# Pacing a chunk inverse on VectorE against other work, and moving one matmul behind the next projection

## The chip, the cores and the metric

The kernel runs on one core of a Trainium2 chip. The metric is device time in microseconds (us) of one execution. The median of three runs is 1108.27 us (1107.01 to 1110.66). The execution that was profiled took 1108.38 us; the span from its first to its last instruction is 1106.6 us.

The engines are named as the profile names them: PE is the matmul engine (PEld its weight loads), DVE the vector engine, ACT the activation engine, POOL and SP the engines that here mostly issue transfers.

## The reference, cut to what matters

One layer of a hybrid encoder over 512 frames of width 1024. Three mixers run side by side (a gated short convolution, a gated linear recurrence, and an RWKV-7 time mixing with 16 heads of 64), their gated sum goes through an output matrix, and a squared-ReLU MLP follows. The part around the change is the RWKV-7 mixer:

```python
kk = heads(k * k_k)
kk = kk / jnp.maximum(jnp.sqrt(jnp.sum(kk * kk, axis=-1, keepdims=True)), 1e-12)
k = k * (1.0 + (a - 1.0) * k_a)
...
sa = jnp.einsum('bhvk,bhk->bhv', state, -kk_t)
state = (state * w_t[:, :, None, :]
         + sa[..., None] * (kk_t * a_t)[:, :, None, :]
         + v_t[..., None] * k_t[:, :, None, :])
y_t = jnp.einsum('bhvk,bhk->bhv', state, r_t)
```

`r`, `k` and `v` are projections of the normalized input, each mixed with its own value one frame earlier (the "token shift"). The sums in the second line are the key norms: one number for each head and frame.

## The kernel before, in words

Matmuls are made in three passes of a two-part split: every weight tile of 128x1024 is loaded by SP (`raw`), cast by ACT to its high part (`whi`, line 147) and subtracted by DVE to its low part (`wlo`, recorded at line 104, as all DVE `tensor_tensor` are). `scalar_tensor_tensor` is recorded at line 107. A projection (`proj`) takes one such weight tile and makes 8 x 3 matmuls of 512 columns (lines 168 to 170) into a bank of the PSUM pool `pp`, which has three. `raw` has two buffers, `whi` and `wlo` three each. Small results go to the PSUM pool `pm`, which has two banks for everything: norm sums `pn`, decay and gate products `pw` and `pa`, and the products `pG`, `pT` and others.

The recurrence is computed in chunks of 64 frames. The 16 heads are worked in four groups of four heads. For each group:

- `krv` (lines 416 to 509) makes the keys, receptances and values. It goes over two pairs of heads (`jj`), and for each it projects the key (`k`), shifts it into `ks`, squares it on ACT into `sq`, splits `sq` into `bh` and `bl`, multiplies them by a block-diagonal matrix of ones into `pn` (lines 433 and 434), and turns `pn` into `kk` by `rsqrt_rows`: a DVE transpose into `rqw` (line 194), some ten tiny operations on `rqq`, a transpose back (line 201) and a multiplication. Then it projects the receptance (`r`) and shifts it into `rs`; then come `pw` (lines 444 and 445), `pa` (450 and 451), a scan over frames, and the tiles `AR` and `BK`, which need `kk`, `rs` and `ks`. After both pairs come two value projections.
- `amat` (lines 515 to 542) multiplies `BK` with `AR` into 64x64 matrices for each chunk and head (`pA`, line 524), masks them into `AXt`, and transposes `BK` (`pB`, line 539).
- `inverse` (lines 544 to 599) inverts the triangular matrices of the group. It transposes two diagonal 32x32 blocks into a layout with one matrix for each partition (line 551, two transposes), then runs 31 dependent steps of two DVE operations each: a product into `dg` and a sum into `Z`. Two transposes bring the blocks back (line 573), one more prepares a left operand (line 578), then 2 x 16 small matmuls `pG` (line 585), 2 x 16 small matmuls `pT` (line 595) with ACT copies after each half, and the result goes to memory as `ttd`.

The order of the work is written out by generators. `weave(crit, fill, r)` advances `crit` by one `yield` and then `fill` by `r` yields on average, until `crit` ends. The critical generator is traced with a raised priority. For groups 1 to 3, `inverse` of the group before is the critical one and `fill_group` the filler; its steps are 22 steps of `ab` (the convolution and linear-recurrence mixers, one projection about every four steps), then the 26 steps of `krv` with 18 more `ab` steps mixed in, and 4 `ab` steps: 70 in all. What is left of them when `inverse` ends is run by `drain`; `amat` follows. The last group's `inverse` has plain `ab` steps beside it, and after it the chain over the chunks begins.

`inverse` yields 2 times before its steps, once after each step, `N_TT` times ahead of each of the three later transposes, `NINV` times ahead of `pG`, once after each half of `pG`, `NG_T` times ahead of `pT` and once after each half of `pT`.

A planner then fixes one order for each engine's queue: among the instructions that its own model takes to be ready it picks the one of highest priority, which is program order less the raise. `tc.keep_in_program_order(x)` ties an instruction to the one traced just before it on its engine, so that the planner cannot place it earlier. On the chip each queue runs in the order so fixed.

The constants are at lines 25, 28 to 31; `rsqrt_rows` at 190 to 201; the step that is tied at 562 to 564.

Of the kernel before, what the change touches and what calls it, by code (L numbers as in the profile page):

```python
# [9 lines left out]
F32 = mybir.dt.float32  # L10
# [8 lines left out]
P = 128  # L19
# [2 lines left out]
CP, CPV, CPI, CPC, CPN = 150, 20, 0, 20, 5  # L22
HOT = 6000

N_TT, NINV, NG_T, N_LOAD = 2, 7, 4, 6


N_KRV = 22
F_INV, F_KRV, F_GAP = 22, 16, 4
W3 = 3  # L30
R0, R1, R2, R3, R4 = 0.85, 0.87, 0.9, 1.7, 1.0
NWARM = 2
POOL_KT = (1, 3, 5, 6, 7)
S = 512
# [64 lines left out]
def block_kernel(ctx, tc, xt, win, par, mulr, sw, wout, w1, w2, fg, cst, eyes, out):  # L99
# [3 lines left out]
    def tt(o, a, b, op):  # L103
        return v.tensor_tensor(out=o, in0=a, in1=b, op=op)  # L104
# [9 lines left out]
    def f(t):  # L114
        return t.bitcast(F32)
# [14 lines left out]
    pv = lambda n, j: part[:, PI[n], j:j + 1]  # L130
# [28 lines left out]
    def split(pool, src, tag, rows=slice(0, P), bufs=None):  # L159
        th, tl = tag if type(tag) is tuple else (tag + "h", tag + "l")  # L160
        hi = pool.tile([P, S], F32R, tag=th, name=th, bufs=bufs)
        lo = pool.tile([P, S], F32R, tag=tl, name=tl, bufs=bufs)
        ac.copy(hi[rows], src)
        tt(lo[rows], src, f(hi[rows]), SUB)
        return hi, lo
# [21 lines left out]
            stt(t, t, -0.5, y, MUL, MUL)  # L187
            stt(y, t, 1.5, y, ADD, MUL)

    def rsqrt_rows(pool, o, ps, low, scale=1.0):  # L190

        w = pool.tile([P, S], F32, tag="rqw", name="rqw")
        q = pool.tile([P, 3, 16], F32, tag="rqq", name="rqq")
        v.transpose(w, ps)
        wv = w.rearrange("p (b j) -> p b j", j=32)[:, :, 0]
        if scale == 1.0:
            v.tensor_scalar(out=q[:, 0], in0=wv, scalar1=low, scalar2=None, op0=MAX)
        else:
            ts2(q[:, 0], wv, scale, low, MUL, ADD)
        rsqrt(q[:, 0], q[:, 1], q[:, 2])  # L200
        v.transpose(o, q[:, 1].unsqueeze(2).to_broadcast([P, 16, 32]))
# [9 lines left out]
    ps = ExitStack()  # L211
# [98 lines left out]
    def proj(name):  # L310
        w = load_w(win[CN[name]])
        t = pp.tile([P, S], F32, tag="pp", name="pp")
        for kt in range(KT):
            wh, wl = wslice(w, kt)
            mm3(t, wh, wl, hh[:, kt], hl[:, kt], start=kt == 0, stop=kt == KT - 1)
            if kt % 2 == 1 and kt < KT - 1:
                yield
        return t
# [5 lines left out]
    def shift(pt, mu, omu, o):  # L324
        ac.activation(o, pt, AF.Copy, scale=omu)
        stt(o[:, 1:], pt[:, 0:S - 1], mu, o[:, 1:], MUL, ADD)
# [3 lines left out]
    pk = pk_ctx.enter_context(tc.tile_pool(name="pk", bufs=1))  # L330
# [24 lines left out]
    OMK, OMR, OKA, OMV, N4, P4, HLG = range(7)  # L355
    v.tensor_scalar(out=dv[:, HLG], in0=part[:, PI["lg"]], scalar1=0.5, scalar2=None, op0=MUL)
    dvp = lambda i, j: dv[:, i, j:j + 1]
# [58 lines left out]
    def krv(g, G_):  # L416
        G_.AR = pk.tile([P, 2, NC, 2, L], F32, tag="AR", name="AR")
        G_.BK = pk.tile([P, 2, NC, 2, L], F32, tag="BK", name="BK")
        vs = [p1.tile([P, S], F32, tag=f"v{h}", name=f"v{h}") for h in range(2)]
        for jj in range(2):  # L420
            j = 2 * g + jj
            rs = WP("rs")
            if j == 0:
                ks = k0
            else:
                ks = WP("ks")
                t = yield from proj(("k", j))
                shift(t, pv("mu_k", j), dvp(OMK, j), ks)
            sq = WP("a1")
            ac.activation(sq, ks, AF.Square, scale=pv("kk", j))  # L430
            sqh, sql = split(pk, sq, "b")
            pn = pm.tile([P, S], F32, tag="pm", name="pn")
            pe.matmul(pn, bd, sqh, start=True, stop=False)
            pe.matmul(pn, bd, sql, start=False, stop=True)
            kk = WP("a5")
            rsqrt_rows(pk, kk, pn, 1e-24)
            stt(kk, ks, pv("kk", j), kk, MUL, MUL)
            yield
            t = yield from proj(("r", j))
            shift(t, pv("mu_r", j), dvp(OMR, j), rs)  # L440
            yield
            swh, swl = load_sw(pk, "swa", j, 0, 2)
            pw = pm.tile([P, S], F32, tag="pm", name="pw")
            pe.matmul(pw, swh[:, 0], lws, start=True, stop=False)
            pe.matmul(pw, swl[:, 0], lws, start=False, stop=True)
            sig = WP("a1")
            ac.activation(sig, pw, AF.Tanh, bias=pv("w0", j), scale=0.5)
            v.tensor_scalar(out=sig, in0=sig, scalar1=1.0, scalar2=None, op0=ADD)
            pa = pm.tile([P, S], F32, tag="pm", name="pa")
            pe.matmul(pa, swh[:, 1], las, start=True, stop=False)  # L450
            pe.matmul(pa, swl[:, 1], las, start=False, stop=True)
            av = WP("a4")
            ac.activation(av, pa, AF.Tanh, bias=pv("a0", j), scale=0.5)
            cum = WP("a2")
            v.tensor_tensor_scan(out=cum, data0=smk, data1=sig, initial=0.0, op0=MUL, op1=ADD)
            PP = pk.tile([P, NC, L + 1], F32, tag="PPt", name="PPt")
            gp.memset(PP[:, :, 0:1], 1.0)
            Pt = PP[:, :, 1:L + 1]
            ac.activation(Pt, c3(cum), AF.Exp, scale=-0.5 * CW)
            v.tensor_copy(PL[:, g, jj], PP[:, :, L])  # L460
            pinv = WP("a3")
            ac.activation(pinv, cum, AF.Exp, scale=0.5 * CW)
            stt(G_.AR[:, jj, :, 0], c3(kk), -1.0, PP[:, :, 0:L], MUL, MUL)
            tt(G_.AR[:, jj, :, 1], c3(rs), Pt, MUL)
            t_ = WP("a1")
            stt(t_, av, 1.0, kk, ADD, MUL)
            stt(G_.BK[:, jj, :, 0], c3(t_), 0.5, c3(pinv), MUL, MUL)
            kp = WP("a2")
            ts2(kp, av, pv("ka", j), dvp(OKA, j), MUL, ADD)
            tt(kp, kp, ks, MUL)  # L470
            tt(G_.BK[:, jj, :, 1], c3(kp), c3(pinv), MUL)

            if jj == 0:
                rk = [WP(f"rk{h}") for h in range(2)]
            for h in range(2):
                r = slice(64 * h, 64 * h + 64)
                stt(rk[h][64 * jj:64 * jj + 64], rs[r], part[r, PI["rk"], j:j + 1], kp[r], MUL, MUL)

        for jj in range(2):
            for h in range(2):  # L480
                gp.dma_start(axd[:, 0:64, g, 0, 2 * h + jj].rearrange("c d t -> d c t"),
                             G_.AR[64 * h:64 * h + 64, jj, :, 0])
            gp.dma_start(rtd[:, :, g, jj].rearrange("c p t -> p c t"), G_.AR[:, jj, :, 1])
        rk = [split(pk, rk[h], ("a1", "a3") if h else "b") for h in range(2)]
        for h in range(2):
            q = 2 * g + h
            t = yield from proj(("v", q))
            shift(t, pv("mu_v", q), dvp(OMV, q), vs[h])
            yield
        for h in range(2):  # L490
            pb = pm.tile([P, S], F32, tag="pm", name="pb")
            for i in range(2):
                pe.matmul(pb, bd, rk[h][i], start=i == 0, stop=i == 1)
            BV[2 * g + h] = [bv_tile(2 * g + h, th) for th in range(2)]
            for th in range(2):
                tt(BV[2 * g + h][th], pb[:, HALF[th]], vs[h][:, HALF[th]], MUL)
        yield
        for b in range(2):
            pt = pm.tile([P, 2, 2, P], F32, tag="pm", name="pV")
            for i in range(2):  # L500
                for h in range(2):
                    pe.transpose(pt[:, i, h], vs[h][:, (2 * b + i) * P:(2 * b + i + 1) * P], ident)
            vt = p1.tile([P, 2, 2, P], F32, tag="vt", name="vt", bufs=2)
            ac.copy(vt, pt)
            for i in range(2):
                c = 2 * (2 * b + i)
                gp.dma_start(vtd[c:c + 2, :, g].rearrange("c s e v -> (c s) (e v)"),
                             vt[:, i].rearrange("p h x -> p (h x)"))
        yield
# [34 lines left out]
    def inverse(g, G_):  # L544
# [12 lines left out]
        for s in range(31):  # L557
            n, c = 31 - s, s + 1
            tv = tmp[:, 0:n * c].rearrange("l (c t) -> l c t", c=c)
            mm = tt(tv, la[:, s, s + 1:32].unsqueeze(1).to_broadcast([64, c, n]),  # L560
                    xt[:, 0:c, s:s + 1].to_broadcast([64, c, n]), MUL)
            if s % 6 == 5:

                tc.keep_in_program_order(mm)
            tt(xt[:, 0:c, s + 1:32], xt[:, 0:c, s + 1:32], tv, ADD)
            yield
# [399 lines left out]
    with tc.tile_pool(name="mw", bufs=2) as mw, \  # L966
# [12 lines left out]
        for fi in range(NF):  # L979
            t = pp.tile([P, S], F32, tag="pp", name="p1")  # L980
            w = load_w(w1[fi])
# [7 lines left out]
            r = mw.tile([P, S], F32, tag="r", name="r")  # L989
# [18 lines left out]
        with tc.tile_pool(name="fin", bufs=1, side="right") as fin:  # L1008
# [15 lines left out]
            for fi in range(NF - 2):  # L1024
                w = load_w(w2[fi])
# [103 lines left out]
```

## Time and profile before

| what | value |
|---|---|
| median of three runs | 1108.27 us |
| profiled execution | 1108.38 us, span 1106.6 us |
| PE busy | 1056.1 us (95% of the span) |
| DVE busy | 743.6 us (67%) |
| ACT busy | 473.9 us (43%) |
| first `amat` begins | 97.8 us |
| second, third, fourth `amat` begin | 222.5, 350.9, 473.0 us |
| last small matmuls of the last `inverse` | 557 to 561 us |

The stretches between those starts are called group 1 (98 to 222.5 us), group 2 (to 350.9) and group 3 (to 473) below; the stretch to 562 us is the last group's. The chain over the chunks and the gates follow to about 676 us, the output matrix to 722 us, and the MLP to the end.

Rows of the view by stretches give the stretch, its length, then busy time and number of instructions for PE, PEld, DVE, ACT and POOL, then the granted PE clock as a share of full speed, the share of the transfer engines and GB/s. Rows of the view of waits read: engine and instruction, what it waited for, idle us in total, times, longest. Rows of the timeline give start, duration, engine, line, operation, tiles, shape and, in brackets, idle time ahead of it and what ended it. Rows of groups give busy us and mean ns of one, then idle time before.

### The profile page before, as it was taken

How to read it: one execution, taken by the hardware profiler on the slowest of the kernel's cores; microseconds unless marked ns; L12 is line 12 of the kernel's file. 1: busy time of each engine (PE TensorE's matmuls, PEld its weight loads, DVE VectorE, ACT ScalarE, POOL GpSimd, SP SyncE). 2: the span in 40 equal slices, each digit the busy share in tenths (PEclk: the TensorE clock that was granted, in tenths of full speed). 3: DMA queues.
4: the chain of work that ended last, by engine and by line, in shares of the span. 5: the costliest groups of instructions: out<-in, count | busy, mean ns of one | idle time of the engine just before them, and what ended most of it. 6: DMA issues, size and time to landing. Idle time of an engine off the chain costs nothing.

```text
span 1106.6 us, 16112 instructions
## 1 busy us (share of the span) xinstructions
PE 1056.1 (95%) x6396; PEld 865.3 (78%) x6396; DVE 743.6 (67%) x1276; ACT 473.9 (43%) x698; POOL 108.9 (10%) x167
## 2 busy tenths in 40 slices
PE   8899979999799989999899999999999999999996
PEld 5677868887588867887687887898888888888885
DVE  7997898879978998769947677955444443222224
ACT  6655445454344534534555444334433333221114
POOL 3211000210011101210022220001000000000001
PEclk9899989999989989999999999999999999999999
DMA  6243623562234623553279773234333335322231
GB/s 209 83 124 98 180 79 113 139 182 86 77 105 129 177 85 96 147 148 106 79 225 281 263 223 101 87 124 153 96 99 98 104 99 191 96 95 95 96 95 76
DMA packets 43324, 142.13 MB, mean 128 GB/s; under 512 B 5681, under 2 KB 9265, under 8 KB 42225
## 3 DMA queue, kind: packets, MB, share of 16 engines
q1 hardware_dynamic: 29472, 91.02, 25.7%
q0 software_dynamic: 13056, 49.03, 15.9%
q8 instruction: 50, 0.82, 0.3%
q10 hardware_dynamic: 720, 1.05, 0.3%
q14 instruction: 26, 0.20, 0.1%
HBM read 115.91 MB, written 25.17 MB: 127 GB/s over the span
## 4 chain that ended last, share of the span: by engine, by line
PE 65%; DVE 21%; DMA 5%; issue 5%; ACT 3%; POOL 1%; SPq 0%; ACTq 0%; POOLq 0%; DVEq 0%
PE pp L168 8%; PE pp L169 7%; PE pp L170 7%; PE acc L170 6%; PE acc L168 6%; PE acc L169 6%; PE p L169 5%; PE p L168 5%; PE p L170 5%; DVE wlo L104 4%; DMA raw<-in_win 3%; DVE dg L104 2%; DVE Z L104 2%; DMA rt<-rtd 1%; DVE u L107 1%
## 5 line engine op out<-in xcount | busy, mean ns | idle before, releaser
L104 DVE TENSOR_TENSOR wlo<-raw,whi 128x1024 fp32r<-128x1024 f32 (+1 forms) x164 | 199.5, 1219 | 249.8 <-ACT whi L147 248.9
L147 ACT CAST whi<-raw 128x1024 fp32r<-128x1024 f32 (+1 forms) x164 | 169.6, 1036 | 326.9 <-PE acc L170 125.1
L168 PE MATMUL pp<-hh,whi 128*128 128x512 f32 x696 | 278.5, 401 | 7.2 <-DVE ks L107 4.6
L170 PE MATMUL pp<-hh,wlo 128*128 128x512 f32 x696 | 277.5, 399 | 7.6 <-DVE wlo L104 7.6
L169 PE MATMUL pp<-hl,whi 128*128 128x512 f32 x696 | 277.4, 399 | 2.8 <-DVE hl L107 2.8
L168 PEld LDWEIGHTS pp<-hh,whi 128*128 128x128 f32 x696 | 133.7, 192 | 38.6 <-DVE ks L107 5.0
L170 PEld LDWEIGHTS pp<-hh,wlo 128*128 128x128 f32 x696 | 133.8, 192 | 37.6 <-DVE wlo L104 9.6
L169 PEld LDWEIGHTS pp<-hl,whi 128*128 128x128 f32 x696 | 133.7, 192 | 30.9 <-DVE hl L107 3.2
L170 PE MATMUL p<-h2h,wlo 128*128 128x512 f32 (+1 forms) x264 | 101.4, 384 | 0.0
L168 PE MATMUL p<-h2h,whi 128*128 128x512 f32 (+1 forms) x264 | 101.3, 384 | 0.0
L169 PE MATMUL p<-h2l,whi 128*128 128x512 f32 (+1 forms) x264 | 101.1, 383 | 0.0
L168 PE MATMUL acc<-whi,ah 128*128 128x512 f32 x256 | 99.6, 389 | 0.0
L169 PE MATMUL acc<-wlo,ah 128*128 128x512 f32 x256 | 99.6, 389 | 0.0
L170 PE MATMUL acc<-whi,al 128*128 128x512 f32 x256 | 99.6, 389 | 0.0
L168 PEld LDWEIGHTS p<-h2h,whi 128*128 128x128 f32 x264 | 49.7, 188 | 9.6
L170 PEld LDWEIGHTS p<-h2h,wlo 128*128 128x128 f32 x264 | 49.6, 188 | 9.7
L169 PEld LDWEIGHTS p<-h2l,whi 128*128 128x128 f32 x264 | 49.6, 188 | 9.5
L170 PEld LDWEIGHTS acc<-whi,al 128*128 128x128 f32 x256 | 48.0, 188 | 10.1
L169 PEld LDWEIGHTS acc<-wlo,ah 128*128 128x128 f32 x256 | 48.0, 188 | 10.0
L168 PEld LDWEIGHTS acc<-whi,ah 128*128 128x128 f32 x256 | 48.0, 188 | 9.8
L104 DVE TENSOR_TENSOR Z<-Z,dg 64x31 f32<-64x31 f32 (+15 forms) x124 | 42.2, 340 | 4.1
L104 DVE TENSOR_TENSOR dg<-Z 64x31 f32<-64x31 f32 (+15 forms) x124 | 42.2, 340 | 4.0
(296 smaller groups left out, 1457.0 us busy)
## 6 DMA issues: line engine op xcount, KB each, us to landing
raw<-in_win SPq DMA_DIRECT2D x88, 512.0 KB, 3.6
raw<-in_w SPq DMA_DIRECT2D x64, 512.0 KB, 3.5
ax<-axd POOLq DMA_DIRECT2D x8, 1024.0 KB, 7.2
axd<-AXt POOLq DMA_DIRECT2D x12, 512.0 KB, 7.2
bkd<-BKT POOLq DMA_DIRECT2D x4, 1024.0 KB, 13.6
raw<-in_wout SPq DMA_DIRECT2D x8, 512.0 KB, 4.3
bk<-bkd POOLq DMA_DIRECT2D x7, 512.0 KB, 8.0
swr<-in_sw SPq DMA_DIRECT2D x16, 128.0 KB, 2.3
```

Source lines behind the costliest of these rows:

```text
L104: return v.tensor_tensor(out=o, in0=a, in1=b, op=op)
L107: return v.scalar_tensor_tensor(out=o, in0=a, scalar=s, in1=b, op0=op0, op1=op1)
L147: ac.copy(hi[:, sl], raw[:, sl])
L168: pe.matmul(ps, wh, xh, start=start, stop=False)
L169: pe.matmul(ps, wh, xl, start=False, stop=False)
L170: pe.matmul(ps, wl, xh, start=False, stop=stop)
```

## The change

`N_TT`, `NINV` and `NG_T` become smaller and the ratios `R1` (groups 1 to 3) and `R2` (last group) larger: `inverse` yields fewer times, and more filler steps go by for each of its yields. In groups 1 to 3 it goes from 54 yields x 0.87 = 47 of the 70 filler steps to 47 x 1.2 = 56; in the last group from 54 x 0.9 = 48.6 to 47 x 1.02 = 47.9. Every third of its 31 steps, instead of every sixth, is tied to program order. In `krv`, the two matmuls `pn` and the `rsqrt_rows` behind them are traced after the receptance's projection and shift instead of ahead of them. `rsqrt_rows` takes the buffer tag of its wide scratch tile as an argument, and `krv` gives it `a3`, which is otherwise `pinv`'s.

```diff
-N_TT, NINV, NG_T, N_LOAD = 2, 7, 4, 6
+N_TT, NINV, NG_T, N_LOAD = 1, 4, 3, 6
-R0, R1, R2, R3, R4 = 0.85, 0.87, 0.9, 1.7, 1.0
+R0, R1, R2, R3, R4 = 0.85, 1.2, 1.02, 1.7, 1.0
-    def rsqrt_rows(pool, o, ps, low, scale=1.0):
+    def rsqrt_rows(pool, o, ps, low, scale=1.0, tag="rqw"):
-        w = pool.tile([P, S], F32, tag="rqw", name="rqw")
+        w = pool.tile([P, S], F32, tag=tag, name="rqw")
...
             sqh, sql = split(pk, sq, "b")
+            yield
+            t = yield from proj(("r", j))
+            shift(t, pv("mu_r", j), dvp(OMR, j), rs)
             pn = pm.tile([P, S], F32, tag="pm", name="pn")
             pe.matmul(pn, bd, sqh, start=True, stop=False)
             pe.matmul(pn, bd, sql, start=False, stop=True)
             kk = WP("a5")
-            rsqrt_rows(pk, kk, pn, 1e-24)
+            rsqrt_rows(pk, kk, pn, 1e-24, tag="a3")
             stt(kk, ks, pv("kk", j), kk, MUL, MUL)
-            yield
-            t = yield from proj(("r", j))
-            shift(t, pv("mu_r", j), dvp(OMR, j), rs)
             yield
...
-            if s % 6 == 5:
+            if s % 3 == 2:
                 tc.keep_in_program_order(mm)
```

## The prediction

> **What bounds the kernel now.** I read the page first, then the view by stretches, to see where PE is not busy.
>
> ```profile
> span 1106.6 us, 16112 instructions
> ...
> PE 1056.1 (95%) x6396; PEld 865.3 (78%) x6396; DVE 743.6 (67%) x1276; ACT 473.9 (43%) x698; POOL 108.9 (10%) x167
> ```
> ```profile
> 98.00:222.50 124.50, 116.50 (x658) 94.52 (x656) 110.44 (x197) 58.42 (x85) 15.05 (x24) 0.97 0.44 123
> 222.50:350.90 128.40, 118.96 (x659) 97.09 (x658) 108.39 (x195) 60.62 (x89) 11.85 (x18) 0.95 0.40 113
> 350.90:473.00 122.10, 117.02 (x659) 95.50 (x658) 104.97 (x188) 54.45 (x78) 14.44 (x22) 0.96 0.45 126
> 473.00:562.00 89.00, 83.14 (x512) 67.01 (x512) 75.65 (x127) 44.27 (x63) 4.11 (x6) 0.98 0.39 114
> 722.00:1092.00 370.00, 370.00 (x1763) 311.30 (x1763) 137.93 (x155) 114.52 (x156) 6.98 (x11) 1.00 0.33 106
> ```
>
> The MLP (last row) has no idle PE and a full clock; nothing there can move. In groups 1 to 3 and the last group PE is idle for 8.0 + 9.4 + 5.1 + 5.9 = 28.4 us, and the clock is below full. DVE is busy for 85 to 89% there, far above its 67% over the span: two engines are near their bound at once. The waits say what PE stood for:
>
> ```profile
> PE pn L433 <- ACT bh L163: 9.4, 4, 5.3
> PE pp L170 <- DVE wlo L104: 7.6, 4, 5.8
> PE pp L168 <- DVE ks L107: 4.6, 1, 4.6
> PE pB L539 <- DVE AXt L104: 1.8, 2, 1.6
> PE pp L168 <- ACT g L797: 1.4, 1, 1.4
> PE pG L585 <- DVE u L789: 1.2, 1, 1.2
> DVE rqw L194 <- PE pn L434: 3.9, 4, 1.4
> ```
>
> The first row names ACT, but the timeline shows that DVE was the late one:
>
> ```profile
> 155.08 0.67 ACT L325 ACTIVATE ks<-pp,dv 128x512 f32<-128x512 f32 x1
> ```
> ```profile
> 110.77 2.11 DVE L551 STREAM_TRANSPOSE Z<-AXt 32x1024 f32<-32x1024 f32 x1
> ...
> 155.85 1.23 DVE L104 TENSOR_TENSOR wlo<-raw,whi 128x1024 fp32r<-128x1024 f32 x1
> 157.11 0.21 DVE L104 TENSOR_TENSOR Z<-Z,dg 64x31 f32<-64x31 f32 x1
> 157.35 1.90 DVE L573 STREAM_TRANSPOSE Z<-Z 32x1024 f32<-32x1024 f32 x1
> 159.28 0.69 DVE L104 TENSOR_TENSOR u<-u,g 128x512 f32<-128x512 f32 x1
> 159.88 0.74 DVE L107 SCALAR_TENSOR_TENSOR ks<-pp,part,ks 128x511 f32<-128x511 f32 x1
> ...
> 163.85 1.23 DVE L578 STREAM_TRANSPOSE dg<-Z 32x1024 f32<-32x1024 f32 x1
> ```
> ```profile
> 162.15 0.80 PE L433 MATMUL pn<-bh,bd 128*128 128x512 f32 x1 [5.34 <-ACT bh L163]
> ```
>
> ACT had its half of the key's shift at 155.75; DVE took it up at 159.88, 4.1 us later, behind the inverse's last step and a transpose. `pn` needs that shift, a square and a cast, so PE stood for 5.34 us. The idle time has a second price, the clock in the stretch right after each stall (PE busy without a break, clock in the column before the last two):
>
> ```profile
> 162.15:168.00 5.85, 5.85 (x16) 4.66 (x17) 5.52 (x16) 2.72 (x4) 0.00 (x0) 0.60 0.00 0
> 279.40:284.00 4.60, 4.60 (x13) 3.70 (x14) 3.75 (x7) 1.53 (x2) 0.00 (x0) 0.63 0.07 27
> 304.82:315.00 10.18, 10.18 (x82) 8.36 (x83) 7.10 (x10) 2.56 (x4) 0.00 (x0) 0.57 0.37 116
> 408.31:414.00 5.69, 5.69 (x16) 4.55 (x17) 5.37 (x11) 1.69 (x3) 0.00 (x0) 0.63 0.54 179
> 438.00:445.00 7.00, 7.00 (x51) 5.50 (x50) 5.88 (x16) 3.24 (x5) 0.71 (x1) 0.76 0.39 76
> 546.60:554.00 7.40, 7.39 (x80) 6.27 (x81) 7.10 (x9) 4.53 (x6) 0.00 (x0) 0.77 0.32 102
> ```
>
> Length times the missing share gives 2.3 + 1.7 + 4.4 + 2.1 + 1.7 + 1.7 = 13.9 us. Groups 1 to 3 thus lose 22.5 us idle, less some 2 us ahead of `pB` and its like that no edit touches, and 12.2 us of clock: 32.7 us are in reach. The last group loses 5.9 + 1.7.
>
> **The change part by part: the spread.** What it moves is DVE work:
>
> ```profile
> L104 DVE TENSOR_TENSOR dg<-Z 64x31 f32<-64x31 f32 (+15 forms) x124 | 42.2, 340 | 4.0
> L104 DVE TENSOR_TENSOR Z<-Z,dg 64x31 f32<-64x31 f32 (+15 forms) x124 | 42.2, 340 | 4.1
> ```
> ```profile
> 175.77 2.14 PE pG L585 x64
> ...
> 222.59 1.99 PE pA L524 x32
> ```
>
> A step is two operations of 0.34 us with some 0.03 us ahead of each (4.0 us / 124): 0.74 us, and 31 steps are 23 us for each group. Two transposes of line 573 and one of line 578 add about 5 us. From the end of the line 551 transposes (112.88) to `pA` (222.59) are 109.7 us for 70 filler steps, 1.57 us each.
>
> Before, step s stands after 0.87 (s + 2) filler steps, so all 31 are through at 28.7, the three transposes at 34. After, the steps end at 33 x 1.2 = 39.6 and the transposes at 43. At filler step 22, where `krv` begins, 23 steps were traced before and 16 will be: 7 x 0.74 = 5.2 us less. At step 35, when the first pair's key and receptance are projected, it is 31 against 27 steps and the three transposes: 3 + 5 = 8 us less DVE work ahead of what PE needs. The stalls in those places are 5.8 us and less. What is late next is the same 8 us, now at steps 36 to 43, beside the second pair. The room for them:
>
> ```profile
> 163.00:222.00 59.00, 59.00 (x361) 47.99 (x361) 51.31 (x93) 31.33 (x45) 9.91 (x16) 0.97 0.44 123
> 313.00:350.00 37.00, 36.73 (x217) 29.80 (x217) 30.02 (x55) 23.24 (x35) 5.13 (x8) 0.99 0.43 118
> ```
>
> DVE idles 7.7 and 7.0 us there; less 0.03 us for each instruction, 4.9 and 5.3 us are usable. So about five of eight fit, not all in the right place. I take half of the 32.7 us as kept, for both edits of groups 1 to 3 together: -16.4 us. Bounds: none of it, if the stalls only move back; or four fifths, -26 us. DVE's own floor does not forbid that: its busy time and the 0.03 us gaps come to 116, 114 and 111 us for stretches of 124.5, 128.4 and 122.1.
>
> The ties make runs of three steps (2.2 us) where six (4.4 us) could stand; a tied step waits behind whatever filler work was traced ahead of it on DVE, and the steps behind it wait too. Nobody waits for those steps before `pG`, so this costs nothing while `pG` has slack. That slack shrinks: `NINV` 7 x 0.87 = 6.1 filler steps become 4 x 1.2 = 4.8, or 2 us less; in group 1 it is 10.7 us (165.08 to 175.77). In the last group 6.3 become 4.1, 3.5 us less, and there PE already waited 1.2 us at `pG`. Between 0 and 2 us in each group and 0 and 3.5 us in the last; I take +1 in all for the former and +2 for the latter. The spread itself is only 12% thinner in the last group (steps end at 33.7 instead of 29.7): -1.5 of its 7.6 us.
>
> **The norm sums.** Removed is PE's wait for the chain shift, square, cast: 9.4 us. Its cover is the receptance's 24 matmuls at 0.23 us, 5.5 us, longer than the longest wait. The cover needs its weights: in group 1 their split ended at 157.08, 0.3 us after PE stopped. This saving is within the half already taken, because DVE is late next. Added is a wait: `pn`, `pw` and `pa` now follow one another at once on the two banks of `pm`, so `pa` waits until DVE has transposed `pn`, and PE's queue stands behind it. Bounds: 0, and the 4.1 us of lag that DVE had at `ks`. The nearest row is `rqw` itself: DVE waited for PE there four times in eight, so it is mostly prompt. I take 0.3 us for eight pairs, +2.4. The `rsqrt_rows` chain is late by a projection, hidden by the value projections between it and `amat`. The tag `a3` costs nothing: its other users come behind `rqw` on DVE's own queue. No transfer is added, and SP's loads keep their traced order (`k`, `r`, the small weights). POOL issues the stores of `AR` later, since `kk` is later; what reads them is loaded only for the chain after 562 us.
>
> **The clock.** The stretch from 438 us stands behind a stall of 0.47 us, that from 546.6 behind those of 1.4 and 1.2 us at `g` and `pG` in the waits, and both have a reduced clock:
>
> ```profile
> 435.92 0.50 PE L433 MATMUL pn<-bh,bd 128*128 128x512 f32 x1 [0.47 <-ACT bh L163]
> ```
>
> So short stalls count too, and halving them gives back about half. The Trainium skill (TensorE: Matmul & The Clock Gate, section "Why this matters for your kernels") says to avoid idle gaps over about 3 us; by that alone, gaps halved to under 3 us would give all the lost clock back. The trace disagrees in the two rows above.
>
> **Sum:** -16.4 - 1.5 + 1 + 2 + 2.4 = -12.5 us on the profiled execution's 1108.38 (0.1 us from the median): 1096 us.
>
> **The rivals.**
> - DVE is the bound: the moved 8 us push stalls from the first pair to the second and to `amat`. For it: 85 to 89% busy. Against it: the usable idle time above. The gain would be 0 to 5 us: 1104 to 1108, say 1106.
> - Slower: `pa` waits for `pn`'s bank. If DVE is as late at `rqw` as it was at `ks`, 4.1 us for the six pairs of groups 1 to 3 is 24.6 us against 14.9 of gain: 1118. It decides from 2.5 us for each pair. Against it: DVE's promptness at `rqw` so far; for it: 8 us more DVE work in that very place.
> - The clock returns whole, because halved stalls no longer trip it: another 6.1 us, 1090. Against it: the two rows above. This is the rule of the Trainium skill cited above.
> - The spread does not happen, since the planner reorders, and only `pn` is moved: half of 9.4 + 4.0, 1102. Against it: 28.7 steps x 1.57 = 45 us, and the steps did take 44.4 us (112.88 to 157.32): program order is followed.
>
> **How the numbers follow.** Forecast 0.47, DVE bound 0.20, slower 0.18, clock 0.08, no spread 0.07. About 0.3% (3.3 us) is what a measurement of this kernel can tell. The forecast, the clock and no spread are faster, and a third of the DVE rival: 0.69; its rest is the same: 0.13; slower 0.18. The range goes from 1082 (the four fifths, with nothing else) to 1113, half-way into the slower rival; about 0.15 is left out. The likeliest case's own range is 1084 to 1104.
>
> **What would show it.** Right: the row of `pn` falls under 2 us in all; from line 551 to the last step some 62 us pass in each group instead of 44; the three stretches shorten to about 119, 121 and 119 us; fewer stretches at half clock. Wrong: a new row of `pa` or `pw` waiting for `rqw` or ACT; waits at `pA` or `AXt` of several us; `pG` waiting for line 578 by more than 2 us; DVE above 95% busy with PE idle as before.

## The result, and the profile after

The changed kernel takes 1116.97 us (median of eight runs, 1110.83 to 1119.52) against 1108.17 us for the kernel before in the same measurement: a ratio of 1.0074 [1.0052, 1.0096]. It is slower by 8.8 us, where 12.5 us less were forecast. The profiled execution took 1118.59 us, with this page:

```profile
span 1116.8 us, 16116 instructions
...
PE 1059.4 (95%) x6396; PEld 867.1 (78%) x6396; DVE 741.9 (66%) x1276; ACT 473.2 (42%) x698; POOL 107.7 (10%) x167
```

The page hides the change: the same work, the same shares. The view by stretches does not. The stretches are again cut at the starts of `amat`, and the last one at the end of the last small matmuls (568.30 us; before, the cut at 562 lies 0.7 us behind that end):

```profile
98.20:227.60 129.40, 121.34 (x659) 97.47 (x658) 110.03 (x197) 58.44 (x85) 15.29 (x25) 0.95 0.41 119
227.60:345.40 117.80, 114.25 (x660) 92.98 (x659) 106.07 (x194) 60.24 (x89) 10.75 (x17) 1.00 0.43 123
345.40:473.80 128.40, 119.98 (x659) 97.47 (x658) 104.36 (x189) 55.03 (x78) 15.14 (x24) 0.93 0.41 120
473.80:568.30 94.50, 82.26 (x504) 66.23 (x503) 75.50 (x127) 42.99 (x62) 4.10 (x6) 0.93 0.36 107
```

Length less the second number is PE's idle time; length times what the clock lacks is the time lost to the clock. Both are worked out so below, for the rows of before too; the clock is given to two places, so a figure of the last column is good to some 0.6 us.

| stretch | length before, after | PE idle before, after | lost to the clock before, after |
|---|---|---|---|
| group 1 | 124.5, 129.4 | 8.0, 8.1 | 3.7, 6.5 |
| group 2 | 128.4, 117.8 | 9.4, 3.6 | 6.4, 0.0 |
| group 3 | 122.1, 128.4 | 5.1, 8.4 | 4.9, 9.0 |
| last group | 89.0, 94.5 | 5.9, 12.2 | 1.8, 6.6 |
| sum | | 28.4, 32.3 | 16.8, 22.1 |

Group 2 gained more than forecast, 10.6 us. Groups 1 and 3 and the last group lost more than that together: the last `amat` begins 375.3 us after the first before, and 375.6 us with the change. The mark for what the last group costs is the chain's first matmul that reads the recurrent state (`py<-St,rt`, line 652), here before and after:

```profile
588.06 1.15 PE L652 MATMUL py<-St,rt 64*64 64x64 f32 x32 [1.54 <-DMA rt<-rtd]
598.04 1.15 PE L652 MATMUL py<-St,rt 64*64 64x64 f32 x32 [1.36 <-DMA rt<-rtd]
```

It comes 115.0 us after the start of the last `amat` before and 124.2 us with the change, so the last group costs 9.2 us; from there to the end both take about the same, 518.5 and 518.8 us. Idle time rose by 3.9 us and lost clock by 5.3, 9.2 us of the 10.2 by which the span grew.

What PE stood for now:

```profile
PE pG L585 <- DVE dg L578: 16.2, 3, 10.8
PE pp L168 <- DVE ks L107: 5.8, 1, 5.8
PE pa L450 <- DVE rqw L194: 3.7, 2, 1.9
...
PE pB L539 <- DVE AXt L104: 1.8, 2, 1.6
PE pn L436 <- ACT bh L163: 1.7, 3, 0.7
```

The rows that led before, `pn` with 9.4 us and `wlo` with 7.6, are down to 1.7 and 1.1 us. In their place leads a row that the kernel before did not have: `pG` waits 16.2 us, 10.8 of them at once, for the transpose of line 578, the last piece of the inverse on DVE. Before, `pG` waited 1.2 us in all, in the last group; its row names `u`, a tiny operation of DVE that ends together with that transpose:

```profile
545.33 1.23 DVE L578 STREAM_TRANSPOSE dg<-Z 32x1024 f32<-32x1024 f32 x1
546.61 2.21 PE L585 MATMUL pG<-dg,AXt 32*32 32x32 f32 x64 [1.16 <-DVE u L789]
```

The timeline of PE in the last group shows the place after the change:

```profile
547.35 0.39 PE L169 MATMUL pp<-hl,whi 128*128 128x512 f32 x1
558.50 3.62 PE L585 MATMUL pG<-dg,AXt 32*32 32x32 f32 x64 [10.76 <-DVE dg L578]
562.04 0.80 PE L170 MATMUL pp<-hh,wlo 128*128 128x512 f32 x1
```

And that of DVE in the same stretch, with the weight split that the projection needs (`wlo` at 545.96), the inverse's last steps (`dg` and `Z`, shapes shrinking to 64x31) and its three transposes:

```profile
535.75 0.32 DVE L104 TENSOR_TENSOR Z<-Z,dg 64x156 f32<-64x156 f32 x1
536.10 0.69 DVE L107 SCALAR_TENSOR_TENSOR u<-u,u 128x512 f32<-128x512 f32 x1
...
545.96 1.20 DVE L104 TENSOR_TENSOR wlo<-raw,whi 128x1024 fp32r<-128x1024 f32 x1
547.07 0.68 DVE L107 SCALAR_TENSOR_TENSOR g<-g,u 128x512 f32<-128x512 f32 x1
547.77 0.30 DVE L104 TENSOR_TENSOR dg<-Z 64x135 f32<-64x135 f32 x1
...
553.11 0.21 DVE L104 TENSOR_TENSOR Z<-Z,dg 64x31 f32<-64x31 f32 x1
553.35 3.83 DVE L573 STREAM_TRANSPOSE Z<-Z 32x1024 f32<-32x1024 f32 x2
557.21 1.23 DVE L578 STREAM_TRANSPOSE dg<-Z 32x1024 f32<-32x1024 f32 x1
```

The inverse stops for 11.7 us in the middle of its steps (536.07 to 547.77) while DVE works on the filler (and idles for some 2.5 us in between), and goes on 0.02 us after a filler operation ends. That step is the 27th, one of those that the change ties. PE has come to `pG` at 547.74 and stands there, in the middle of a projection: line 170, which follows `pG` in its queue, has had its weights since 547.16. The Trainium skill (PSUM — Partial Sum Buffer, section "Engine vs sequencer instructions") says that matmuls start and complete in program order; the trace agrees, for the ready matmul ran at 562.04, behind all of `pG`.

Each such stall is followed by a reduced clock, again with PE busy nearly throughout (the first two rows; the third holds the rest of the stall at `ks` as well, the fourth that of 2.56 us at `pG`):

```profile
193.70:206.00 12.30, 12.28 (x114) 9.86 (x115) 7.76 (x21) 4.56 (x8) 0.68 (x1) 0.60 0.05 12
558.50:566.00 7.50, 7.50 (x103) 6.39 (x103) 4.19 (x6) 1.87 (x3) 0.55 (x1) 0.58 0.31 107
398.20:408.00 9.80, 4.03 (x11) 3.24 (x11) 9.36 (x19) 1.71 (x3) 0.00 (x0) 0.65 0.23 69
432.70:442.00 9.30, 6.74 (x72) 5.57 (x72) 7.72 (x11) 4.32 (x7) 0.00 (x0) 0.63 0.42 144
```

The first row stands behind a wait of 2.84 us at `pG` in group 1 and costs 4.9 us of clock (12.3 x 0.40): more than the wait itself, and as much as the whole of group 1 grew by.

### The profile page after: what moved, and what is told of

It reads as the page before. It is cut to its first block, busy times and chain, and to the rows that moved or that the text cites. A ratio compares the mean times of both kernels' runs of the same rounds, so it can differ in the third digit from the quotient of the medians.

```text
span 1116.8 us, 16116 instructions
## 1 busy us (share of the span) xinstructions
PE 1059.4 (95%) x6396; PEld 867.1 (78%) x6396; DVE 741.9 (66%) x1276; ACT 473.2 (42%) x698; POOL 107.7 (10%) x167
## 4 chain that ended last, share of the span: by engine, by line
PE 62%; DVE 23%; DMA 5%; issue 5%; ACT 3%; POOL 1%; SPq 0%; DVEq 0%; ACTq 0%; POOLq 0%
PE acc L169 7%; PE pp L168 7%; PE acc L170 7%; PE acc L168 7%; PE pp L169 6%; PE pp L170 6%; PE p L170 5%; PE p L169 5%; PE p L168 5%; DVE wlo L104 5%; DVE dg L104 3%; DVE Z L104 3%; DMA rt<-rtd 2%; DMA raw<-in_win 2%; DVE Z L573 1%
## 6 DMA issues: line engine op xcount, KB each, us to landing
swr<-in_sw SPq DMA_DIRECT2D x16, 128.0 KB, 2.2
```

## The experiments

After the result there were two theories for the 10.8 us. The first: the tie of every third step holds the inverse behind filler work that was traced ahead of it, so DVE finishes late. The rival: the thinner pace (larger ratio, fewer yields) sets `pG` too early against DVE, whatever the ties. Beside them stood the question what the norm sums' move is worth by itself. All ratios below are to the kernel before, measured beside each run on the same chip; "the old settings" are those of before.

### The parts by themselves: the norm sums

The kernel before, with only the norm sums moved.

```diff
# the changed kernel, with the settings of before
+N_TT, NINV, NG_T, N_LOAD = 2, 7, 4, 6
+R0, R1, R2, R3, R4 = 0.85, 0.87, 0.9, 1.7, 1.0
+            if s % 6 == 5:
```

> The kernel before with only the norm sums moved behind the receptance; all constants and ties as before. Theory 1 and 2: the waits at pn (9.4 us) go, some of it comes back elsewhere: 1098 to 1106 us. Theory 3 (PE waits at pa for pn's bank): 1112 us or more, with waits at pa of over 8 us in all.

Measured: 1107.17 us, 0.999 [0.9976, 1.0004]: no difference that counts, though the wait that it aims at is gone. Its leading waits:

```profile
PE pa L450 <- DVE rqw L194: 5.8, 3, 3.2
PE pp L168 <- DVE ks L107: 5.2, 2, 4.6
```

With the old pace the waits at `pn` and `wlo` go (1.9 and 1.8 us are left), and others come: `pa` behind `pn`'s bank takes 5.8 us where there was none, and `pG` 2.2 us for the transpose of line 578. `ks` keeps its place. The three groups last 124.0, 128.0 and 122.0 us, within half a microsecond of before.

### The parts by themselves: the spread

The kernel before with the change's constants and ties, the norm sums left in their old place; and the same for groups 1 to 3 alone, with the last group as before.

```diff
# spread only, on the kernel before
+N_TT, NINV, NG_T, N_LOAD = 1, 4, 3, 6
+R0, R1, R2, R3, R4 = 0.85, 1.2, 1.02, 1.7, 1.0
+            if s % 3 == 2:
# spread in groups 1 to 3 only, on the kernel before
+R0, R1, R2, R3, R4 = 0.85, 1.2, 0.9, 1.7, 1.0
+        N_TT, NINV, NG_T = (2, 7, 4) if g == NG - 1 else (1, 4, 3)
+            if (s % 6 == 5) if g == NG - 1 else (s % 3 == 2):
```

> The changed constants and ties, with the norm sums where they were before. Theory 1 and 2: the wait at pG in the last group stays about 10 us, time 1114 to 1122 us. Theory 3: no loss, 1108 us or less.

> The kernel before with only groups 1 to 3 spread (yields 1, 4, 3, ratio 1.2, every third step tied); last group and norm sums as before. If the two edits work on the same stalls independently: 1109 to 1112 us (the norm sums alone gave 1 us). If the spread needs the moved norm sums, because the key's chain now competes with the inverse for longer: 1115 to 1120 us, with waits of several us at pn in groups 1 and 3.

Measured: 1127.37 us, 1.0172 [1.0149, 1.0194], and 1118.27 us, 1.0071 [1.0055, 1.0088]. Without the moved norm sums the spread saves nothing. The waits of PE in the second of these:

```profile
PE pn L433 <- ACT bh L163: 8.3, 5, 4.3
PE pp L170 <- DVE wlo L104: 6.8, 5, 4.6
PE pp L168 <- DVE ks L107: 6.5, 1, 6.5
```

`pn` and `wlo` keep 8.3 and 6.8 us of their 9.4 and 7.6. So the two edits are not additive: the norm sums' move is worth 1 us alone (inside its interval), and 9 to 11 us beside the spread (1.0071 against the 0.9992 of the next experiment; 1.0172 against the whole change's 1.0074).

### Where the loss sits: the last group

The whole change, with the last group's inverse wholly as before; and the kernel before, with only the last group's inverse as changed.

```diff
# last group old, on the changed kernel
+R0, R1, R2, R3, R4 = 0.85, 1.2, 0.9, 1.7, 1.0
+        N_TT, NINV, NG_T = (2, 7, 4) if g == NG - 1 else (1, 4, 3)
+            if (s % 6 == 5) if g == NG - 1 else (s % 3 == 2):
# last group new, on the kernel before
+R0, R1, R2, R3, R4 = 0.85, 0.87, 1.02, 1.7, 1.0
+        N_TT, NINV, NG_T = (1, 4, 3) if g == NG - 1 else (2, 7, 4)
+            if (s % 3 == 2) if g == NG - 1 else (s % 6 == 5):
```

> The changed kernel with everything of the last group's inverse as before (yields 2, 7, 4, ratio 0.9, every sixth step tied); groups 1 to 3 and the norm sums as changed. If the last group alone holds the loss (theory of the last group): its wait at pG of 10.8 us falls to about 1 us, the chain starts some 9 us sooner, time 1105 to 1109 us. If the loss is spread over the groups: 1112 us or more.

> The kernel before with only the last group's inverse as changed (yields 1, 4, 3, ratio 1.02, every third step tied); norm sums and groups 1 to 3 as before. Theory of the last group: PE waits about 10 us at pG there, time 1116 to 1120 us. If the loss is spread over the groups: within 3 us of 1108.

Measured: 1108.97 us, 0.9992 [0.9978, 1.0006]; and 1118.94 us, 1.0071 [1.005, 1.0092]. The whole loss against before goes with the last group's new settings, and comes with them alone: there `pG` waits 10.8 us, as in the changed kernel (the profile of that run is of its shortest execution, 1113.19 us). With the last group old, `py` of line 652 comes 115.7 us behind the last `amat` (115.0 before, 124.2 with the change). What is left for groups 1 to 3 is nought: group 2's gain against the losses of the other two.

### Ties or pace

Four kernels. The whole change with the old ties (every sixth step); the whole change with the tie of the 27th step alone taken off in the last group; the last group with its old pace but the new ties (the rest as changed); and the whole change with the ties of the 25th and later steps, and those of the three transposes behind them, taken off.

```diff
# ties of before
-            if s % 3 == 2:
+            if s % 6 == 5:
# the 27th step loose
+            if s % 3 == 2 and not (g == NG - 1 and s == 26):
# last group: old pace, new ties
+R0, R1, R2, R3, R4 = 0.85, 1.2, 0.9, 1.7, 1.0
+        N_TT, NINV, NG_T = (2, 7, 4) if g == NG - 1 else (1, 4, 3)
# the whole tail loose
+            if s % 3 == 2 and s < 24:
-            tc.keep_in_program_order(v.transpose(TT[...], xt[...]))
+            v.transpose(TT[...], xt[...])
-        tc.keep_in_program_order(v.transpose(d1[0:32], TT[0:32, :, 0:32]))
+        v.transpose(d1[0:32], TT[0:32, :, 0:32])
```

> The changed kernel with the ties of before (every sixth step). Theory 1 (the tie): in the last group step 27 (the 5x27 product) is tied behind the gelu and scan block of the filler, 12 us late, and PE stands 10.8 us at pG and then runs some 10 us at half clock. With every sixth step tied that step is loose: the wait at pG in the last group falls under 2 us, and the time to 1102 to 1107 us. Theory 2 (the yields): pG comes too early because there are fewer yields ahead of it, whatever the ties: its wait in the last group stays over 6 us and the time over 1112. Theory 3 (the norm sums): the loss is at pn, pw and pa: the time stays at 1117.

> The changed kernel with one tie taken out: step 27 (the 5x27 product) of the last group; the order on the vector engine's queue is the changed kernel's up to that step. Theory 1: the whole loss of the last group is that tie: steps 27 to 31 and the three transposes end about 10 us earlier, PE's wait at pG there falls from 10.8 to under 2 us, the half clock behind it goes or is short, time 1102 to 1106 us. Theory 2: the wait at pG stays over 5 us and the time over 1111. Theory 3: 1117, as the changed kernel.

> The changed kernel with the last group's yields and ratio as before (2, 7, 4 and 0.9), every third step tied everywhere. PE's order is that of the run with the last group all old; only DVE's differs. If pace makes the last group's loss: the transposes are early again, wait at pG under 3 us, 1107 to 1111 us. If the ties alone make it: an early tied step stands behind a filler block, the inverse ends up to 8 us later, PE waits over 5 us at pG, 1113 or more.

> The changed kernel with the ties of the 25th and later steps and of the three later transposes taken out. Theory of the ties: the last steps and the transposes no longer stand behind filler work, the transpose of line 578 ends 5 to 12 us earlier, PE's waits at pG are under 3 us in all, time 1100 to 1107 us. Theory of the distance: the loose transposes are still placed by the planner near their traced place, the waits stay over 8 us in all, time 1112 or more.

Measured, in that order: 1114.94 us, 1.0058 [1.0039, 1.0078]; 1117.42 us, 1.0083 [1.0057, 1.0109]; 1120.7 us, 1.0088 [1.007, 1.0106]; 1105.38 us, 0.9954 [0.9938, 0.997].

With the old ties `pG` in the last group still waits 8.9 us, and `py` comes 124.3 us behind the last `amat`. So the first theory fell as it stood: the closer ties are not needed for the loss. There the steps end at 537.71, but the transpose of line 578, which was tied before the change too, starts only at 550.47. With only the 27th step loose it is the same: the steps end at 540.3, 13 us sooner than with the change, and the transpose of line 578 starts at 553.10:

```profile
540.13 0.21 DVE L104 TENSOR_TENSOR Z<-Z,dg 64x31 f32<-64x31 f32 x1
540.37 1.95 DVE L573 STREAM_TRANSPOSE Z<-Z 32x1024 f32<-32x1024 f32 x1
...
545.41 1.95 DVE L573 STREAM_TRANSPOSE Z<-Z 32x1024 f32<-32x1024 f32 x1
...
553.10 1.23 DVE L578 STREAM_TRANSPOSE dg<-Z 32x1024 f32<-32x1024 f32 x1
```

`pG` waits 8.9 us there: one tie taken off, and the next one of the same kind is what is late. The rival theory fell as well: at the old pace the new ties alone lose as much (`py` comes after 125.3 us), with the third step stuck behind a filler operation whose block waits for a late transfer (`swr`):

```profile
488.38 0.22 DVE L104 TENSOR_TENSOR Z<-Z,dg 64x60 f32<-64x60 f32 x1
...
497.97 0.29 DVE L104 TENSOR_TENSOR swcl<-swr,swch 128x128 fp32r<-128x128 f32 x1 [6.43 <-ACT swch L406]
...
506.12 0.74 DVE L107 SCALAR_TENSOR_TENSOR g<-g,part,g 128x510 f32<-128x510 f32 x1
506.89 0.25 DVE L104 TENSOR_TENSOR dg<-Z 64x87 f32<-64x87 f32 x1
```

From 488.6 to 506.89 the inverse does not move, and DVE idles 6.43 us of that; `pG` waits 9.9 us at the end. In the kernel before, the steps went on around the same wait (at 491.54 its sixth step was done). With the whole tail loose the loss turns into a gain: line 578 starts at 540.71 there, and `pG` waits 6.2 us, since the planner now also places it earlier, at 535.8. The gain is that of groups 1 to 3, which take 368.7 us from the first `amat` to the last (375.3 before); the last group is still 5.3 us above before.

The times of the last group, in us from the start of its `amat`, show which side moved:

| kernel | PE comes to `pG` | line 578 ends | wait at `pG` | `py` of line 652 |
|---|---|---|---|---|
| before | 72.4 | 73.5 | 1.2 | 115.0 |
| the change | 73.9 | 84.6 | 10.8 | 124.2 |
| ties of before | 72.0 | 80.9 | 8.9 | 124.3 |
| the 27th step loose | 72.1 | 80.9 | 8.9 | 125.4 |
| old pace, new ties | 71.8 | 81.6 | 9.9 | 125.3 |
| the whole tail loose | 69.1 | 75.2 | 6.2 | 120.3 |

In the four kernels that lose all of it, PE is where it was to within 1.5 us, and DVE is 7 to 11 us later. Loosening the tail brings DVE back to within 2 us; what is left of the wait are these 2 us and PE coming 3.3 us sooner. So either of the two, closer ties or the thinner pace, is enough, and what they have in common is this: a tied piece of the inverse stands on DVE behind a filler block, and PE has `pG` placed for an inverse that is not held up.

### Where PE comes to `pG`

If that is the mechanism, `pG` traced later should cost less where the place follows the trace. The whole change with `NINV` 7 as before; the same for groups 1 to 3 with the last group wholly as before; and this last with the tail's ties off in groups 1 to 3.

```diff
# NINV 7 throughout
-N_TT, NINV, NG_T, N_LOAD = 1, 4, 3, 6
+N_TT, NINV, NG_T, N_LOAD = 1, 7, 3, 6
# NINV 7, last group old
+R0, R1, R2, R3, R4 = 0.85, 1.2, 0.9, 1.7, 1.0
+        N_TT, NINV, NG_T = (2, 7, 4) if g == NG - 1 else (1, 7, 3)
+            if (s % 6 == 5) if g == NG - 1 else (s % 3 == 2):
# the same, tail loose in groups 1 to 3 (the three transposes too)
+            if (s % 6 == 5) if g == NG - 1 else (s % 3 == 2 and s < 24):
```

> The changed kernel with 7 yields instead of 4 ahead of pG; nothing else. Theory of the distance (pG stands too soon behind the transpose that it needs): pG comes 3.6 filler steps (5.6 us) later in groups 1 to 3 and 3 steps (4.9 us) later in the last, so its waits of 2.8, 2.6 and 10.8 us become 0, 0 and about 6, the half clock behind the first two goes, time 1106 to 1111 us. Theory of the ties (the transpose itself is late by its ties, and PE has no other work that late): the last wait stays at 8 us or more and the time at 1114 or more.

> Groups 1 to 3 as changed but with 7 yields ahead of pG; the last group as before; norm sums moved. If the waits at pG in groups 1 and 3 (2.9 and 2.5 us with 4 yields, and the half clock behind them) are what the spread still costs there, they are gone: 1101 to 1105 us. If what holds those groups is DVE's lag elsewhere (ks, wlo): 1107 to 1110, as with 4 yields (1109).

> As the run with 7 yields ahead of pG in groups 1 to 3 and the last group as before, and with the ties of the 25th and later steps and of the three transposes taken out in groups 1 to 3. If the ties at the inverse's end still cost something there: below that run by 2 to 5 us, 1097 to 1102. If not: the same within 2 us.

Measured: 1111.55 us, 1.0016 [1.0003, 1.0029]; 1103.74 us, 0.9938 [0.9923, 0.9953]; 1104.55 us, 0.9944 [0.9923, 0.9965]. Three yields more ahead of `pG` in groups 1 to 3 are worth 0.9992 less 0.9938, 6 us. The row of `pG` waiting for the transpose is gone from the second kernel's waits, and others lead:

```profile
PE pp L168 <- DVE ks L107: 7.0, 2, 6.4
PE pn L437 <- DVE bl L104: 4.1, 3, 2.3
```

Its four stretches add up to 458.5 us, against 464.0 before and 470.1 with the change:

```profile
97.50:223.90 126.40, 118.69 (x659) 95.00 (x658) 109.18 (x197) 58.65 (x85) 15.05 (x25) 0.97 0.42 121
223.90:341.70 117.80, 114.27 (x661) 92.81 (x660) 106.96 (x195) 61.08 (x89) 11.67 (x19) 1.00 0.44 124
341.70:467.60 125.90, 117.21 (x661) 94.81 (x660) 103.32 (x188) 54.42 (x78) 14.23 (x22) 0.96 0.43 121
467.60:556.00 88.40, 82.51 (x510) 66.52 (x510) 75.65 (x127) 43.72 (x63) 4.10 (x6) 0.98 0.40 115
```

In groups 1 and 3 the clock is 0.97 and 0.96, where the change has 0.95 and 0.93. This version beats both kernels, but its gain over before is all in group 2: groups 1 and 3 are still 1.9 and 3.8 us longer than before. With `pG` late enough, loosening the tail's ties adds nothing: the two last intervals lie on each other. In groups 1 to 3, DVE's lateness at the inverse's end costs only where PE comes to its result too soon.

In the last group `NINV` 7 did not change the wait: 10.8 us are left.

```profile
554.73 1.49 PE L585 MATMUL pG<-dg,AXt 32*32 32x32 f32 x24 [10.81 <-DVE dg L578]
```

PE comes to `pG` 73.9 us behind the last `amat` here (470.05 to 543.92), as in the changed kernel (473.82 to 547.74): it stands at the same place, three yields or not. The first matmul of `pG` is not tied, so the planner is free to place it earlier than it was traced. Why the yields move it in groups 1 and 3 and not here stays open.

## Why the prediction was wrong

**What bounds the kernel** was read rightly: PE's waits for DVE in groups 1 to 3 and the half clock behind them. **The gain of the spread and the norm sums** is there in group 2, at 117.8 us where 121 were forecast, with its lost clock gone; the row of `pn` fell to 1.7 us (0.5 us more are at its second matmul). In groups 1 and 3 it is not: even in the kernel with the late `pG` they take 126.4 and 125.9 us, where 119 were forecast for each. The wait at `ks` in group 3, 4.6 us before, stayed (5.8 us with the change, 6.4 there), and `pn`'s second matmul in group 1 now waits 2.3 us for `bl`. So with `pG` out of the way both edits brought 6.9 us (0.9938) in groups 1 to 3, where 14.0 (-16.4 and +2.4) were forecast: that sum was about twice too large, because part of the stalls only moved back, which the forecast had as its other bound. Not foreseen was that neither edit brings anything alone; the forecast took them as one sum, which hid that.

**The step that failed**, and that turned a gain into a loss, is the sentence on the ties and `pG`: "Nobody waits for those steps before `pG`, so this costs nothing while `pG` has slack", with +1 us for groups 1 to 3 and +2 for the last group. The wait at `pG` grew by 15 us in all, and the clock behind it comes on top. The forecast counted `pG`'s place on PE well and DVE's badly. In group 1 it put line 578 at 43 filler steps of 1.57 us and `pG` about 4.8 steps later; behind the end of line 551 at 113.35 that makes 181 and some 188. PE came to `pG` at 190.9. DVE came to line 578 at 192.44, 11 us late:

```profile
161.44 0.25 DVE L104 TENSOR_TENSOR Z<-Z,dg 64x87 f32<-64x87 f32 x1
...
182.07 0.22 DVE L104 TENSOR_TENSOR dg<-Z 64x60 f32<-64x60 f32 x1
...
187.68 4.12 DVE L573 STREAM_TRANSPOSE Z<-Z 32x1024 f32<-32x1024 f32 x2
...
192.44 1.23 DVE L578 STREAM_TRANSPOSE dg<-Z 32x1024 f32<-32x1024 f32 x1
```

The 30th step is a tied one, and for 20 us before it DVE works only on the filler, which here is mostly `krv`'s first pair. It was tied before, too, but there it was traced at filler step 27 (31 yields x 0.87), and now at 37 (31 x 1.2), behind that pair's key and receptance. The forecast gave every filler step the mean of 1.57 us; a tied step waits for what stands ahead of it, and that is lumpy. From line 551 to the last step 73 us passed (113.35 to 186.39), not 62.

**The sizes.** Forecast and profiled execution are 22.7 us apart. Groups 1 to 3 were forecast at -13.0 us and came out at +0.3; of these 13 us about 5 are `pG`'s (6 by the run with the late `pG`, where 1 was forecast), and most of the rest is the gain taken too large. In the last group the spread was credited with 1.5 us and `pG` charged with 2, bounds 0 to 3.5. It lost 9.2 us, 8.7 more than the sum of the two. The bound was worked out from the yields alone, as if DVE's pace were what the ratio says; but before, line 578 ended at 546.56, and PE had only 1.2 us to wait there. A forecast that sees a result arrive just in time has no slack to lend, and its upper bound should have been the length of a filler block, which the timeline after shows at some 12 us, plus the clock.

**The rivals.** The slower one named the wrong wait: `pa` behind `pn`'s bank costs 3.7 us, near the 2.4 taken, not 25; that its 1118 us lies next to the measured 1117 is luck. DVE as the bound did not come about: in the four stretches its busy time fell from 399.5 to 396.0 us (it was 84 to 89% before) while they grew from 464.0 to 470.1, so it stood idle for longer, and no wait at `pA` or `AXt` grew. But its picture of stalls that move back is what groups 1 and 3 show. The clock's full return happened in group 2, where idle time fell to 3.6 us, and in no other stretch of the table. By the rule of the Trainium skill cited in the prediction the gaps of 2.84 and 2.56 us should have been harmless; the stretches behind them ran at 0.60 and 0.63, so the trace again disagrees. No spread: it happened.

**The list of what would show it wrong** held the right item, "`pG` waiting for line 578 by more than 2 us", and no chance was attached to it. It should have been the slower rival.

## What to carry to other kernels

When the producer of an operand is slowed down or tied to other work, find the instruction that waits for it on the in-order engine and compare the two times in the trace before, not the slack in counted steps: here 1.2 us of wait were already there. Charge a tie with the whole block that may stand ahead of it, not with the mean of a step. And where one edit moves a wait from one matmul to the next and another edit moves the work behind it, time them apart and together: here neither was worth anything alone, and in groups 1 to 3 the two together were not either until `pG` came later.

## What the runs showed of the hardware

The clock's loss does not grow with the stall. Behind 2.84 us at `pG` in group 1 it was 4.9 us (12.3 us at 0.60), behind 10.76 us in the last group 3.2 us (7.5 us at 0.58). In the kernel with the late `pG`, the same small matmuls of group 1 run from 195.47 at 0.99, with no stall right ahead of them. A stall of 2.34 us at `pn` ends 3.7 us earlier there, at 191.76; the reduced clock behind it lasts for the 512-column matmuls in between and is over when `pG` begins:

```profile
191.80:195.40 3.60, 3.60 (x9) 2.35 (x9) 3.60 (x8) 1.78 (x3) 0.00 (x0) 0.57 0.00 0
195.40:207.00 11.60, 11.60 (x130) 9.37 (x129) 8.49 (x20) 6.68 (x10) 0.89 (x1) 0.99 0.30 81
```

So the small matmuls alone do not bring the reduced clock; a stall right ahead of them does. In the rows shown, it lasts 3.6 to 5.9 us where only 512-column matmuls follow the stall (this row, and the prediction's rows from 162.15, 279.40 and 408.31) and 7.5 to 12.3 us where the 32x32 matmuls of `pG` come first or soon (193.7, 558.5 and, before, 304.82). That is a comparison of rows and not an experiment, so what sets the length stays open. Nor does every short stall bring it: in group 2 PE waited 1.86, 0.91 and 0.70 us, each alone, and the clock of that stretch is 1.00.
